# A hybrid decoder layer: pointwise and output weights joined, q stacked in halves of the partitions

## The chip, the cores and the metric

The kernel runs on one core of one Trainium2 chip. The metric is the device time of one execution in microseconds (us). The three runs of the kernel before took 2022.71, 2019.04 and 2021.59 us, a median of 2021.59. A core has five engines with a queue each: TensorE (PE, matmuls), VectorE (DVE), ScalarE (ACT), GpSimd (POOL) and SyncE (SP, which here only issues DMAs). ACT and POOL issue some DMAs as well.

## The reference

x is 2048 tokens by 1024 channels, float32. In short:

```python
hn   = rms_norm(x, mix_pre_g)
proj = hn @ w_in                     # q 512, k 128, v 128, conv input 2 x 512
attn = sliding_window_attention(q, k, v, sinks, rel_bias)   # 8 q heads, 2 kv heads of 64, window 128
h    = a * sigmoid(gate)             # conv input
h    = causal_depthwise_conv(h, 31 taps) + bias
conv = silu(layer_norm(h)) @ w_conv_pw                      # 512 x 512
mixed = concat(attn, conv) @ w_out                          # 1024 x 1024
h    = x + rms_norm(mixed, mix_post_g)
ff   = (silu(hn2 @ w_gate) * (hn2 @ w_up)) @ w_down         # hn2 = rms_norm(h), width 2816
out  = h + rms_norm(ff, ffn_post_g)
```

## The kernel before

**Matmuls.** Every large product is made of three matmuls. An operand is split into a high part (an ACT copy to the fp32r type, `act(w[:, 0], ...)`) and a low part (the difference, on DVE or POOL), and the product is high x high + high x low + low x high. The helper `three` (L188) issues them; `hl(tag)` (L64) makes a tile of 128 x 2 x 512 for the pair. All matmuls go through the helper `mat` (L107), so their profile line is L108; DVE operations go through `dve` (L83) and have line L85. Groups are therefore told apart by tile names: the letter after the @ is the stage.

**Stages.** Tokens are worked in four tiles of 512. For tile t:

- A (`stage_a`, L327): the input projection, 14 units of 24 matmuls each: eight for the conv input, then k (unit 8), v (9) and four pairs of q heads (10 to 13). Each unit loads 512 KB of w_in and, from tile 1 on, the stored low part (`lo_in`). k goes to `kz` (one buffer, high and low part of the last 128 and the present 512 tokens), q to `ql` tiles. The two kv groups lie in the two halves of the partitions.
- B (`stage_b`, L430): attention, four blocks of 128 tokens. For the scores, `front` issues twelve matmuls per block and pair of head pairs: 64 rows each, three products for each of two heads and two groups, the groups alternating between the two halves of the partitions. The sums lie in `tr` banks of PSUM.
- C (`stage_taps`, L563; `stage_tail`, L577; `conv_tail`, L592): 31 conv taps on DVE, then layer norm, swish and the pointwise product: the conv output is split (L618, L619), w_pw is loaded and split once per tile of tokens, 4 x 12 matmuls run in the single `ct` bank, and the result goes to `mixT` in DRAM by ACT's queue (L631).
- W (`stage_w`, L697): the output projection from `mixT` and w_out, then the norm and the residual (`norm_w`, L747).
- H, F, G: transposes and Strassen-like sums (`stage_h_sums`, L842) and the feed-forward (`stage_pre`, `stage_p1`, `stage_p2`) for two pairs of tiles.

**Order.** The tile framework schedules the instructions in a simulated time by priority (the written order) and sets all semaphores. Written order comes from generators. The main one runs stage after stage; beside it run lanes (`Lane`, L1275) that are given credit for each step of the main one: lb has attention, lc the taps, lw W0 and later C2, W2, C3, W3, ld the tails C0 and C1, lh the sums. A lane's entry can have a condition, such as a stage having started. In A1, hooks at certain units load the next tile's x, compute the row norms of tiles 2 and 3 (`row_norms`, L264, eight loads into `hl` buffers and eight ACT squares, hook at unit 2), turn the norm (L306, L308, tag `gb`) and split the next input (`split_x`, L311, units 10 and 11, eight `hl` tiles for tile 2).

**Buffers.** `BUFS` (L53) gives the buffers of each tag; a new tile waits until the tile that had its buffer is no longer read. Of interest here: wx 1, gb 2, hl 8, chl 5, fc 3, ql 4, w 6, raw 2; in PSUM mm 4, tr 3, ct 1.

Of the kernel before, what the change touches and what calls it, by code (L numbers as in the profile page):

```python
# [37 lines left out]
def layer_kernel(ctx, tc, x, xT, cols, rows, sinks, relb, onehot, w_in, w_pw, w_out, w_gate, w_up, w_down, out):  # L38
# [14 lines left out]
    BUFS = dict(x=4, p=4, wx=1, gb=2, hl=8, ql=4, chl=5, mid=4, mb=2, fa=4, at=2, fc=3, glu=2, yt=1, raw=2, w=6, vd=2)  # L53
# [10 lines left out]
    def hl(tag):  # L64
        return t_(tag, (P, 2, T), F32R)
# [165 lines left out]
    h_scr = dr.tile([S, D], F32, name="h_scr")  # L231

# [7 lines left out]
    kz = cst.tile([P, 2, P + T], F32R, name="kz")  # L240
    nc.gpsimd.memset(kz[:, :, 0:P].bitcast(F32), 0.0)
    junk = cst.tile([P, D], BF16, name="junk")
# [21 lines left out]
    def row_norms(ts, tag):  # L264
        lab[0] = f"A{ts[0]}"
        n = 4 * len(ts)
        ssq = sm(n)
        for i in range(n):
            xt = f4(tag)
            r0 = ts[0] * T + i * P  # L270
            nc.sync.dma_start(xt, x[r0 : r0 + P])
            act(junk, xt, AF.Square, accum_out=ssq[:, i : i + 1])
        r = rsqrt(ssq, n, D)
        for j, t in enumerate(ts):
            rn[t] = r[:, 4 * j : 4 * j + 4]
# [51 lines left out]
    def stage_a(t, hn, before_kv, hooks, post=None):  # L327
# [60 lines left out]
        if t:  # L388
            act(kz[:, :, 0:P], kz[:, :, T : T + P].bitcast(F32), AF.Copy)
# [4 lines left out]
        act(kz[:, 0, P:], ok, AF.Copy)  # L394
        vtt(kz[:, 1, P:], ok, kz[:, 0, P:].bitcast(F32), ALU.subtract)
# [11 lines left out]
        for i in range(4):  # L407
            oq = proj(10 + i)
            if i == 0:
                pv = mm()  # L410
                for s in range(4):
                    nc.tensor.transpose(pv[:, s * P : (s + 1) * P], vt[:, s * P : (s + 1) * P], ident)
                if t:
                    nc.vector.tensor_copy(vtok[:, 0], vtok[:, 4])
                nc.vector.tensor_copy(vtok[:, 1:5].rearrange("p a b -> p (a b)"), pv)
            qi = hl("ql")
            if post:
                qt = f2("fa")
                stt(qt, oq, 0.125, rb, ALU.mult, ALU.mult)
                act(qi[:, 0], qt, AF.Copy)  # L420
                vtt(qi[:, 1], qt, qi[:, 0].bitcast(F32), ALU.subtract)
            else:
                act(qi[:, 0], oq, AF.Copy, scale=0.125)
                stt(qi[:, 1], oq, 0.125, qi[:, 0].bitcast(F32), ALU.mult, ALU.subtract)
            q.append(qi)
            yield 5.2
            step(10 + i)
        qs[t] = q

    def stage_b(t):  # L430
# [3 lines left out]
        def front(b):  # L434
# [6 lines left out]
            for ip in range(2):  # L441
                os = [tr().rearrange("p (j k) -> p j k", j=2) for _ in range(2)]
                lead = []
                for j in range(2):
                    i = 2 * ip + j
                    for n, (a, k) in enumerate(((0, 0), (0, 1), (1, 0))):
                        for g in (1, 0):
                            sl = slice(64 * g, 64 * g + 64)
                            r = mat(os[g][:, j], q[i][sl, a, tok], kz[sl, k, win], start=n == 0, stop=n == 2)
                            if lead:  # L450
                                after_first(lead[-1], r)
                            if len(lead) < 2:
                                lead.append(r)
# [138 lines left out]
    def conv_tail(t, yt):  # L592
# [14 lines left out]
        sc = []  # L607
        for c in range(4):
# [8 lines left out]
            h = hl("chl")  # L617
            act(h[:, 0], v, AF.Copy)  # L618
            ptt(h[:, 1], v, h[:, 0].bitcast(F32), ALU.subtract)  # L619
            sc.append(h)  # L620
            yield 2
            lab[0] = L
        for m in range(4):
            raw = f2("fc")
            nc.sync.dma_start(raw, w_pw[m])
            w = split_w(raw, "mb" if t == 1 and m % 2 else "chl").rearrange("p a (k c) -> p a k c", c=P)
            o = ct()
            three(o, [((w[:, 0, k], w[:, 1, k]), (sc[k][:, 0], sc[k][:, 1])) for k in range(4)])
            z = f2("gb" if t > 1 else "fc")
            act(z, o, AF.Copy, scale=0.5)  # L630
            nc.scalar.dma_start(mixT[4 + m, :, t * T : (t + 1) * T], z)  # L631
            yield 2
            lab[0] = L
# [63 lines left out]
    def stage_w(w, spill, G, atag, htag, mtag, bank_of, norm=None, ready=None):  # L697
# [25 lines left out]
        for gi in range(KC // G):  # L723
            aa = nxt
            for n in range(2):
# [5 lines left out]
                ws = weight(w_out[2 * gi : 2 * gi + 2, :, n * T : (n + 1) * T].rearrange("c p t -> p c t"),  # L731
# [14 lines left out]

    def norm_w(w, spill, acc, mtag):  # L747
# [3 lines left out]
        ssq = sm(4)  # L751
# [4 lines left out]
        r = rsqrt(ssq, 4, D, w < 3)  # L756
        yield 3
        lab[0] = L
        ssq2 = sm(4)
        for s in range(4):  # L760
# [14 lines left out]
            act(junk, acc[s], AF.Square, accum_out=ssq2[:, s : s + 1])  # L775
            yield 5.0
        lab[0] = L
        r2 = rsqrt(ssq2, 4, D, w < 3)
# [586 lines left out]
    lw.add("W0", stage_w(0, True, 2, "x", "hl", "fa", mm), lambda: "A3" in started and "C0" in ld.done)  # L1365
    TGA = [["hl"] * 8, ["mid"] * 4 + ["chl"] * 4, ["hl"] * 8, ["mid"] * 4 + ["hl"] * 4]
# [138 lines left out]
```

## Time and profile before

| What | Value |
|---|---|
| Median of the runs | 2021.59 us |
| Profiled execution, first to last instruction (span) | 2016.4 us |
| Mean granted TensorE clock | 0.991 |
| Matmuls | 8826 |
| Moved by DMA | 451.44 MB, mean 224 GB/s |

The page gives no other time for the profiled execution than its span; what lies around it, by the median of the runs, is 5.2 us. Busy time is the union of an engine's records. A matmul's record is longer than its share of a dense stream, so the price of a matmul is taken from how many run in a stretch without a gap. In the view by groups the columns are: busy us, mean ns of one, idle us just before, and what ended the idle time. In the stretches each engine has its busy us and number of instructions, then come the granted clock, the share of the 16 DMA engines and GB/s. In the view of DMA issues the last two columns are KB each and us from issue to landing.

### The profile page before, as it was taken

To read this page: it belongs to the slowest core of one execution; us is meant where nothing else is said; L and a number is where in the kernel's file an instruction comes from. 1 tells how busy PE (TensorE), PEld (TensorE's weight loads), DVE (VectorE), ACT (ScalarE), POOL (GpSimd) and SP (SyncE) were. 2 spreads that over 40 slices of the span, in tenths; PEclk is the share of its full clock that TensorE was granted. 3 is DMA by queue.
4 is the path that set the end of the run, shared out by engine and by line. 5 is a ranking of instruction groups with operands and counts; after the bars stand their busy time and mean duration, and the time that the engine had idled before them with its cause. 6 is when DMAs were issued, how large, how long until landed. Compare 5 with 4: busy or idle time off the path is not lost. (4 is left out here: it accounts for less than half of the span.)

```text
span 2016.4 us, 27154 instructions
## 1 busy us (share of the span) xinstructions
PE 1957.8 (97%) x8826; PEld 1563.3 (78%) x8826; DVE 1489.5 (74%) x2679; ACT 985.7 (49%) x1938; POOL 355.0 (18%) x415
## 2 busy tenths in 40 slices
PE   8999999999998999999989999999899999999998
PEld 7877767677667778888878878778688888888886
DVE  5998987985794899888569984475766765545558
ACT  5455455457546633333355466456643343345543
POOL 6000223322110300000001022103523332221000
PEclk9999999999999999999989999999999999999999
DMA  8786645669559878777476778579944443366654
GB/s 309 267 298 221 207 148 175 194 228 322 180 178 325 281 238 269 253 253 254 149 239 216 238 261 283 173 262 348 333 159 167 157 160 107 107 238 214 200 187 162
DMA packets 234110, 451.44 MB, mean 224 GB/s; under 512 B 23496, under 2 KB 49264, under 8 KB 233968
## 3 DMA queue, kind: packets, MB, share of 16 engines
q1 hardware_dynamic: 211184, 411.96, 60.9%
q10 hardware_dynamic: 20544, 30.42, 4.1%
q0 software_dynamic: 2240, 7.34, 0.9%
q8 instruction: 69, 1.13, 0.2%
q14 instruction: 73, 0.60, 0.1%
HBM read 330.60 MB, written 119.02 MB: 223 GB/s over the span
## 5 line engine op out<-in xcount | busy, mean ns | idle before, releaser
L85 DVE SCALAR_TENSOR_TENSOR fc@C<-glu@C,colt,fc@C 128x512 f32<-128x512 f32 x480 | 367.8, 780 | 3.0
L108 PE MATMUL mm@F<-hl@H,w@F 128*128 128x512 f32 x1056 | 254.9, 392 | 5.3 <-ACT mm@F L924 4.9
L108 PEld LDWEIGHTS mm@F<-hl@H,w@F 128*128 128x128 f32 x1056 | 198.5, 189 | 48.8 <-ACT mm@F L924 6.7
L108 PE MATMUL mm@G<-hl@G,hl@G 128*128 128x512 f32 x924 | 228.0, 396 | 6.4 <-DVE x@G L85 4.3
L108 PE MATMUL mm@A<-hl@A,w@A 128*128 128x512 f32 x840 | 206.3, 396 | 3.0 <-ACT hl@A L318 1.2
L108 PEld LDWEIGHTS mm@G<-hl@G,hl@G 128*128 128x128 f32 x924 | 174.1, 190 | 44.5 <-issue 4.1
L797 ACT ACTIVATE w@F<-chl@F 128x512 fp32r<-128x512 f32 x220 | 135.6, 625 | 135.3 <-PE mm@F L108 123.3
L108 PE MATMUL mm@G<-w@G,hl@G 128*128 128x512 f32 x876 | 199.5, 389 | 0.0
L108 PEld LDWEIGHTS mm@G<-w@G,hl@G 128*128 128x128 f32 x876 | 164.4, 188 | 34.1
L108 PEld LDWEIGHTS mm@A<-hl@A,w@A 128*128 128x128 f32 x840 | 154.7, 188 | 39.4 <-DVE hl@A L85 3.0
L85 DVE TENSOR_TENSOR w@F<-chl@F,w@F 128x512 fp32r<-128x512 f32 x198 | 144.9, 733 | 34.7 <-ACT w@F L797 34.3
L108 PE MATMUL mm@F<-mid@H,w@F 128*128 128x512 f32 x528 | 131.1, 393 | 7.4 <-ACT mm@F L924 7.2
L108 PE MATMUL mm@F<-p@H,w@F 128*128 128x512 f32 x528 | 129.1, 389 | 0.8 <-ACT at@F L1046 0.8
L108 PE MATMUL mm@F<-ql@H,w@F 128*128 128x512 f32 x528 | 127.2, 389 | 0.7 <-ACT w@F L797 0.7
L108 PE MATMUL mm@F<-x@H,w@F 128*128 128x512 f32 x528 | 125.5, 391 | 0.0
L108 PEld LDWEIGHTS mm@F<-mid@H,w@F 128*128 128x128 f32 x528 | 98.3, 188 | 30.2 <-ACT mm@F L924 9.0
L108 PEld LDWEIGHTS mm@F<-p@H,w@F 128*128 128x128 f32 x528 | 98.9, 188 | 21.9 <-ACT at@F L1046 1.4
L108 PEld LDWEIGHTS mm@F<-ql@H,w@F 128*128 128x128 f32 x528 | 99.0, 188 | 21.6 <-ACT w@F L797 1.1
L108 PEld LDWEIGHTS mm@F<-x@H,w@F 128*128 128x128 f32 x528 | 98.7, 188 | 21.0
L108 PE MATMUL tr@W<-w@W,ql@W 128*128 128x512 f32 x384 | 103.0, 408 | 8.4 <-ACT ql@W L706 5.1
L133 ACT ACTIVATE w@A<-raw@A 128x512 fp32r<-128x512 f32 x110 | 67.7, 626 | 78.8 <-PE mm@A L108 51.5
L108 PE MATMUL mm@W<-w@W,hl@W 128*128 128x512 f32 x384 | 101.5, 404 | 2.2 <-ACT x@W L679 0.7
(302 smaller groups left out, 3337.0 us busy)
## 6 DMA issues: line engine op xcount, KB each, us to landing
mids<-fa@F SPq DMA_DIRECT2D x154, 256.0 KB, 2.7
raw@A<-w_in SPq DMA_DIRECT2D x55, 512.0 KB, 4.4
w@A<-lo_in SPq DMA_DIRECT2D x84, 256.0 KB, 3.5
fc@G<-mids SPq DMA_DIRECT2D x77, 256.0 KB, 3.5
fa@G<-mids SPq DMA_DIRECT2D x75, 256.0 KB, 4.5
gb@F<-keeps SPq DMA_DIRECT2D x72, 256.0 KB, 4.3
raw@W<-w_out SPq DMA_DIRECT2D x32, 512.0 KB, 5.5
w@W<-lo_out SPq DMA_DIRECT2D x48, 256.0 KB, 4.4
```

The source lines that it names most:

```text
L85: r = op(*args, **kw)
L108: r = nc.tensor.matmul(*args, **kw)
L133: act(w[:, 0], raw, AF.Copy)
L797: act(w[:, 0], x, AF.Copy)
```

## The change

Three things change, with what they need in buffers.

1. **Joined weights.** The conv output is no longer multiplied by w_pw tile by tile. A new stage J, in lane ld ahead of C0 and from the start of A1 on, computes 0.5 x w_pw x (rows 512 to 1023 of w_out) once, into `w_join` in DRAM; W reads it in place of these rows. The tails store the swish output itself in `mixT`, by SP's queue. (The host passes w_pw transposed.)
2. **Stacked q.** k and q are split into a staging tile and then copied by SP's DMAs: of each head of q the high part lies in partitions 0 to 63 and the low part in 64 to 127 (`qi`), and k is held in both halves (`kk`). A score is then two matmuls of 128 rows (k high, k low) instead of three of 64; it also contains low x low. The staging tiles use the tag wx (one buffer) for tiles 0 and 1 and chl for 2 and 3.
3. **Buffers.** chl has 4 instead of 5; `junk` has half the columns, so squares of 1024 columns come in two halves and their sums are added (`row_squares`).

```diff
-    BUFS = dict(..., chl=5, ...)
+    BUFS = dict(..., chl=4, ...)
...
+    w_join = dr.tile([4, P, D], F32, name="w_join")
...
-    kz = cst.tile([P, 2, P + T], F32R, name="kz")
+    kk = cst.tile([P, 2, 2, P + T], F32R, name="kk")
-    junk = cst.tile([P, D], BF16, name="junk")
+    junk = cst.tile([P, T], BF16, name="junk")
...
@@ row_norms
-            act(junk, xt, AF.Square, accum_out=ssq[:, i : i + 1])
+            act(xt, xt, AF.Square, accum_out=ssq[:, i : i + 1])
@@ stage_a, unit 8
-        act(kz[:, 0, P:], ok, AF.Copy)
-        vtt(kz[:, 1, P:], ok, kz[:, 0, P:].bitcast(F32), ALU.subtract)
+        kn = hl(TQ[t])
+        act(kn[:, 0], ok, AF.Copy)
+        vtt(kn[:, 1], ok, kn[:, 0].bitcast(F32), ALU.subtract)
+        for g in range(2):
+            for half in range(2):
+                nc.sync.dma_start(kk[64 * half : 64 * half + 64, g, :, P:].bitcast(F32), kn[64 * g : 64 * g + 64].bitcast(F32))
@@ stage_a, units 10 to 13
-            qi = hl("ql")
+            qn = hl(TQ[t])
...
+            qi = hl("ql")
+            for g in range(2):
+                for half in range(2):
+                    nc.sync.dma_start(qi[64 * half : 64 * half + 64, g].bitcast(F32), qn[64 * g : 64 * g + 64, half].bitcast(F32))
@@ stage_b, front
-                lead = []
-                for j in range(2):
-                    i = 2 * ip + j
-                    for n, (a, k) in enumerate(((0, 0), (0, 1), (1, 0))):
-                        for g in (1, 0):
-                            sl = slice(64 * g, 64 * g + 64)
-                            r = mat(os[g][:, j], q[i][sl, a, tok], kz[sl, k, win], start=n == 0, stop=n == 2)
...
+                for g in range(2):
+                    for j in range(2):
+                        for k in range(2):
+                            mat(os[g][:, j], q[2 * ip + j][:, g, tok], kk[:, g, k, win], start=k == 0, stop=k == 1)
@@ conv_tail
-            h = hl("chl")
-            act(h[:, 0], v, AF.Copy)
-            ptt(h[:, 1], v, h[:, 0].bitcast(F32), ALU.subtract)
-            sc.append(h)
+            nc.sync.dma_start(mixT[4 + c, :, t * T : (t + 1) * T], v)
             yield 2
             lab[0] = L
+
+    def stage_join():
+        lab[0] = "J0"
+        right = []
+        for k in range(4):
+            raw = f4("wx", (P, 2, T))
+            nc.sync.dma_start(raw, w_out[4 + k].rearrange("p (a b) -> p a b", a=2))
+            yield 1.5
+            for n in range(2):
+                lab[0] = "J0"
+                right.append(split_w(raw[:, n], "hl"))
+            yield 1.5
...
         for m in range(4):
-            raw = f2("fc")
+            if m % 2 == 0:
+                pair_ = t_("yt", (P, 2, 2, T), F32R)
+            raw = f2("gb")
             nc.sync.dma_start(raw, w_pw[m])
-            w = split_w(raw, "mb" if t == 1 and m % 2 else "chl").rearrange("p a (k c) -> p a k c", c=P)
-            o = ct()
-            three(o, [((w[:, 0, k], w[:, 1, k]), (sc[k][:, 0], sc[k][:, 1])) for k in range(4)])
-            z = f2("gb" if t > 1 else "fc")
-            act(z, o, AF.Copy, scale=0.5)
-            nc.scalar.dma_start(mixT[4 + m, :, t * T : (t + 1) * T], z)
...
+            left = split_w(raw, pair_[:, m % 2]).rearrange("p a (k c) -> p a k c", c=P)
+            yield 1.5
+            for n in range(2):
+                lab[0] = "J0"
+                o = ct()
+                three(o, [((left[:, 0, k], left[:, 1, k]), (right[2 * k + n][:, 0], right[2 * k + n][:, 1])) for k in range(4)])
+                z = f2("gb")
+                act(z, o, AF.Copy, scale=0.5)
+                nc.scalar.dma_start(w_join[m, :, n * T : (n + 1) * T], z)
+                yield 4
...
@@ stage_w
-                ws = weight(w_out[2 * gi : 2 * gi + 2, :, n * T : (n + 1) * T].rearrange("c p t -> p c t"),
+                src = w_out[2 * gi : 2 * gi + 2] if gi < 2 else w_join[2 * gi - 4 : 2 * gi - 2]
+                ws = weight(src[:, :, n * T : (n + 1) * T].rearrange("c p t -> p c t"),
...
@@ norm_w
+    def row_squares(x, ssq, s):
+        for n in range(2):
+            act(junk, x[:, n * T : (n + 1) * T], AF.Square, accum_out=ssq[:, 4 * n + s : 4 * n + s + 1])
...
-            act(junk, acc[s], AF.Square, accum_out=ssq[:, s : s + 1])
+            row_squares(acc[s], ssq, s)
...
@@ main
+    TQ = ["wx", "wx", "chl", "chl"]
...
+    ld.add("J", stage_join(), lambda: "A1" in started)
     for t in range(2):
         ld.add(f"C{t}", stage_tail(t), lambda t=t: since(lc, f"T{t}", CS))
```

More of the change, by code (lines that the diff above doesn't have):

```diff
@@ L51, in nm @@
         return f"{s}@{lab[0]}_{uid[0]}"
-    BUFS = dict(x=4, p=4, wx=1, gb=2, hl=8, ql=4, chl=5, mid=4, mb=2, fa=4, at=2, fc=3, glu=2, yt=1, raw=2, w=6, vd=2)
+    BUFS = dict(x=4, p=4, wx=1, gb=2, hl=8, ql=4, chl=4, mid=4, mb=2, fa=4, at=2, fc=3, glu=2, yt=1, raw=2, w=6, vd=2)
     def t_(tag, shape, dt=F32):
@@ L388, in stage_a @@
         if t:
-            act(kz[:, :, 0:P], kz[:, :, T : T + P].bitcast(F32), AF.Copy)
+            act(kk[:, :, :, 0:P], kk[:, :, :, T : T + P].bitcast(F32), AF.Copy)
         if post:
@@ L774, in norm_w @@
             nc.sync.dma_start(h_scr[r0 : r0 + P], acc[s])
-            act(junk, acc[s], AF.Square, accum_out=ssq2[:, s : s + 1])
+            row_squares(acc[s], ssq2, s)
             yield 5.0
         lab[0] = L
-        r2 = rsqrt(ssq2, 4, D, w < 3)
+        vtt(ssq2[:, 0:4], ssq2[:, 0:4], ssq2[:, 4:8], ALU.add)
+        r2 = rsqrt(ssq2[:, 0:4], 4, D, w < 3)
         yield 3
@@ L1479 @@
     wo = f(w_out)[np.concatenate([pair(i) for i in range(4)] + [np.arange(512, 1024)])]
-    wp = kblocks(f(w_conv_pw))
+    wp = kblocks(f(w_conv_pw).T)
     args = [
```

28 lines of the change are left out of this document (13 added, 15 removed).

## The prediction

> **What bounds the kernel now.** I read the page's head first, then busy time by stretches.
>
> ```profile
> span 2016.4 us, 27154 instructions
> PE 1957.8 (97%) x8826; PEld 1563.3 (78%) x8826; DVE 1489.5 (74%) x2679; ACT 985.7 (49%) x1938; POOL 355.0 (18%) x415
> ```
>
> ```profile
> core 0: us, PE busy (x) PEld busy (x) DVE busy (x) ACT busy (x) POOL busy (x), PEclk, DMA share, GB/s
> 95.50:120.00 24.50, 24.50 (x123) 18.36 (x122) 23.97 (x59) 15.38 (x37) 1.51 (x4) 1.00 1.02 389
> 120.00:192.00 72.00, 72.00 (x357) 55.21 (x357) 63.88 (x158) 33.56 (x87) 5.44 (x12) 1.00 0.73 236
> 192.00:309.00 117.00, 114.12 (x561) 84.40 (x560) 104.70 (x236) 63.39 (x168) 24.34 (x27) 0.99 0.55 175
> 473.00:533.00 60.00, 55.95 (x268) 38.18 (x266) 33.31 (x93) 39.66 (x90) 9.22 (x8) 0.97 0.66 228
> 1027.00:1290.00 263.00, 256.37 (x1131) 209.23 (x1132) 198.43 (x319) 145.82 (x258) 39.46 (x64) 0.99 0.73 240
> 1380.00:1460.00 80.00, 72.75 (x331) 58.85 (x331) 54.82 (x93) 51.28 (x98) 35.77 (x25) 1.00 0.98 349
> ```
>
> TensorE (PE) is busy 97% of the span: 58.6 us are idle in all. The stretches hold the second input stage (A1, 95.5 to 192), the third (A2), the conv tail of tile 1 beside W1 (473 to 533), the tails of tiles 2 and 3 beside W2 and W3 (1027 to 1290) and the feed-forward start with its DMA at 0.98 (1380 to 1460). PE is full or nearly full in each place where the change takes PE work away, so work taken from PE is time, as long as nothing new starves it. In A1 PE never rests, although the 16 DMA engines are saturated in its first 24.5 us; that is the place to watch. The price of a matmul comes from the chain and from PE's own timeline:
>
> ```profile
> 1451.94 343.02 PE mm@F L108 x1512
> ```
>
> ```profile
> 97.21 0.38 PE L108 MATMUL tr@B<-kz,ql@A 64*128 64x256 f32 x1
> 97.52 1.43 PE L108 MATMUL mm@A<-mid@A,w@A 128*128 128x512 f32 x5
> ...
> 112.68 0.97 PE L108 MATMUL tr@B<-kz,ql@A 64*128 64x256 f32 x12
> 113.58 2.56 PE L108 MATMUL mm@A<-chl@A,w@A 128*128 128x512 f32 x10
> ...
> 191.86 0.60 PE L558 MATMUL ct@C<-ident,fc@C 128*128 128x128 f32 x4
> 192.21 6.17 PE L108 MATMUL mm@A<-hl@A,w@A 128*128 128x512 f32 x26
> ```
>
> A full-array matmul of 512 columns takes 343.02 / 1512 = 0.227 us of PE in a dense stream; one of 128 columns (192.21 - 191.86) / 4 = 0.088. Durations of single records (about 0.39) overlap and are not used.
>
> **The change, part by part.**
>
> ```profile
> L108 PE MATMUL ct@C<-chl@C,chl@C 128*128 128x512 f32 x168 | 46.4, 417 | 1.8 <-ACT chl@C L133 1.2 <-POOL chl@C L135 0.6
> L108 PE MATMUL ct@C<-chl@C,mb@C 128*128 128x512 f32 x24 | 6.6, 410 | 0.7 <-POOL mb@C L135 0.6
> L108 PE MATMUL tr@B<-kz,ql@A 64*128 64x256 f32 x384 | 45.7, 310 | 0.1
> L85 DVE SCALAR_TENSOR_TENSOR fc@C<-glu@C,colt,fc@C 128x512 f32<-128x512 f32 x480 | 367.8, 780 | 3.0
> L619 POOL TENSOR_TENSOR chl@C<-fc@C,chl@C 128x512 fp32r<-128x512 f32 x16 | 24.8, 1548 | 106.3 <-ACT chl@C L618 95.3 <-PE ct@C L611 11.0
> L133 ACT ACTIVATE w@A<-raw@A 128x512 fp32r<-128x512 f32 x110 | 67.7, 626 | 78.8 <-PE mm@A L108 51.5 <-DMA raw@A<-w_in 20.1 <-DMA lo_in<-w@A 2.6
> ```
>
> *Pointwise product removed.* 192 matmuls go. Floor: 192 x 0.227 = 43.6 us. Ceiling: their busy and idle time, 46.4 + 1.8 + 6.6 + 0.7 = 55.5, because in the tails PE also waits for the splits on ScalarE (ACT) and GpSimd (POOL) inside these groups. I take 48, nearer the floor, since half of them lie in 1027 to 1290, where PE is busy for 256 of 263 us. The splits of the conv outputs and of w_pw, the 16 loads of w_pw and the scaled copies go too; ACT and POOL are under half busy, so this is nothing.
>
> *Join added.* 4 row blocks x 2 halves x 12 = 96 matmuls: 21.8 us by 0.227, 27.8 by 55.5 / 192 = 0.289. I take 23: A1 is a dense stream, but each chain uses the one ct bank. Net of both: 25 us less (16 to 34).
>
> *Scores.* 384 matmuls of 64 rows become 256 of 128 rows, 256 columns. Before: 45.7 us of PE. In a run of twelve, 113.58 - 112.68 = 0.90 us; one alone costs 0.31. After, each lies between half of 0.227 (0.113) and the line through 0.088 at 128 columns and 0.227 at 512 (0.134): 29 to 34 us; I take 0.12, so 31, nearer the half since PE streams at a constant rate per column. The 45.7 runs into the next matmul by 0.07 at the end of each run (0.97 against 0.90); with 32 runs or more that takes off some 2: a gain of 13 (10 to 15). Against twelve in a run, eight at 0.12 cost 0.96 and gain nothing; the gain lies in the broken runs.
>
> By the Trainium skill, "TensorE: Matmul & The Clock Gate", Part 3, matmuls in different row groups run at the same time, so 192 pairs should have cost 192 x 0.113 = 22 us and the full-array form, at 29, would lose 7; the row of twelve (0.15 per pair) bears this out only in part. "TensorEngine Tiling (Array Packing)", Tiling Modes, says that a change of tiling mode drains the engine, which fits the 0.31 of the single one and goes with the change.
>
> *Copies of q and k.* Each of 4 k and 16 q tiles now goes through a staging tile and four DMAs on the sync queue (SP): 80 issues, 12 MB.
>
> ```profile
> 90.97 0.33 SPq L271 DMA_DIRECT2D hl@A<-x  x1
> ...
> 93.72 1.78 SPq L132 DMA_DIRECT2D w@A<-lo_in  x1
> ```
>
> ```profile
> SPq L132 <- PE mm@A L108: 139.2, 61, 6.5
> ```
>
> ```profile
> raw@A<-w_in SPq DMA_DIRECT2D x55, 512.0 KB, 4.4
> hl@A<-x SPq DMA_DIRECT2D x8, 512.0 KB, 9.2
> mixT<-gb@C ACTq DMA_DIRECT2D x8, 256.0 KB, 4.1
> fc@C<-w_pw SPq DMA_DIRECT2D x16, 256.0 KB, 4.6
> ```
>
> An issue holds SP for 0.33 us: 20 per input stage are 6.6 us. SP already stands 139.2 us waiting for PE to free weight buffers, 46 in each of the three stages that load stored low parts, so it has room; what is queued behind a copy is the next weight loads, and PE holds up to two projections (11 us) in hand. The copies land 4.4 to 9.2 us later than the old in-place split; attention of a tile is a side lane of the next stage, which covers it. In tiles 0 and 1 the staging tile is a single buffer: copy, low part and landing, 0.63, at most a tap's 0.78 and 4.4, 5.8 us, against 24 x 0.227 = 5.4 per projection, and PSUM's four banks cover the difference. 16 stores of the conv output move from ACT's queue to SP (5.3 us of issues), less 12 loads of w_pw. Together I take a loss of 4 (0 to 12).
>
> *Norms.* The squares of W come in halves: 32 more ACT passes of about the split's 0.63, beside PE work; nothing, unless N3 is late, and its lane gets shorter by two tails.
>
> *The ring of hl in A1.* The join holds all eight hl buffers until its last chains; the row norms of tiles 2 and 3 use the same ring, and so does the split of A2's input.
>
> ```profile
> 94.39 1.04 ACT L272 ACTIVATE junk<-hl@A 128x1024 bf16<-128x1024 f32 x1
> ...
> 115.17 1.06 ACT L272 ACTIVATE junk<-hl@A 128x1024 bf16<-128x1024 f32 x1 [1.03 <-DMA hl@A<-x]
> ...
> 164.49 0.59 ACT L308 ACTIVATE gb@A<-mm@A 128x512 f32<-128x512 f32 x1
> 166.59 1.29 ACT L322 ACTIVATE hl@A<-x@A 128x512 fp32r<-128x512 f32 x2 [1.51 <-DVE x@A L85]
> ...
> 173.35 0.62 ACT L322 ACTIVATE hl@A<-x@A 128x512 fp32r<-128x512 f32 x1
> ```
>
> Now the split ends at 174 and A2 starts at 192: 18 us of slack. After, A1 ends at 192 + 22 - 3 = 211. The join: its first load needs the staging buffer, free after A0's last q copy, about 95.5 + 5.8 = 101; four w_out pairs, each a load (4.4), an ACT split (0.63) and two POOL subtractions (1.5 each, L619's row) = 8.0, end at 133. Four row blocks, each a load (4.6), a split (2.2), two chains with copies (2 x 3.3) and a store (4.1) that must land before the two-buffer gb ring turns, 14 to 17.5: the end at 189 to 203. With A2's eight splits (7.4) that is 196 to 211, just in time; but the loads fall into the saturated stretch, where landings cost 9.2, and the norm of A2 shares gb. I take 9 us of PE idle at A2's start (0 to 20).
>
> *One chl buffer fewer.* The Strassen sums before the feed-forward use three a step; the stall beside them is
>
> ```profile
> L108 PE MATMUL mm@F<-mid@H,w@F 128*128 128x512 f32 x528 | 131.1, 393 | 7.4 <-ACT mm@F L924 7.2
> ```
>
> 7.4 us over both pairs of tiles; a step that has to wait for a buffer adds to that. I take 4 more (0 to 8, the same again).
>
> **Sum.** -25 - 13 + 4 + 9 + 4 = -21 us on this execution's span of 2016.4, so 1995.4. The runs' median is 2021.59, 5.2 above the span; that stays: 2000.6, said as 2000.
>
> **The rivals.** *The norms stand behind the join.* If the join gets hl first, the row norms start only as it ends: 189 to 203, plus the eight squares (94.4 to 116.2, 21.8) and from the copied norm to the last split 164.5 to 174 (9.5): 220 to 234 against 211. The stall is about 20 instead of 9: 2011. For it: the join is first in the written order. Against it: the x rows are issued at 90.97, while A0 still runs, whenever a buffer frees, and the join's first split waits for the staging buffer.
>
> *Row groups already run side by side.* Then scores lose 7 instead of gaining 13: 2000 + 20 = 2020, no change. Against it stands 45.7, which is 0.24 per pair.
>
> *The copies hold the weights back (slower).* A copy waits in SP for the low part on VectorE (DVE), which stands behind conv taps.
>
> Two taps of 0.78, the low part and the ACT copy are 2.9 us; five tiles a stage, 14.5, plus 6.6 of issues, are 21, in four stages 84. SP's 46 us of standing in a stage cover this on average. The uncovered share decides: at 30% (25 of 84, the gain of 21 and the 4 already charged) the gain is gone. Half uncovered is 42 where the sum has 4: 38 more, 2038. For it: the DMA is saturated at A1's start. Against it: PE has weights for 11 us in hand, and one tile's hold is 2.9 + 4 x 0.33 = 4.2.
>
> **How the numbers follow.** Forecast 0.55, own range 1978 to 2010; norms behind the join 0.15; row groups 0.08; copies 0.22, a third of it in the partial form that only eats the gain. Faster: 0.55 + 0.15 + 0.03 of the row groups + 0.02 of the copies = 0.75. Within 0.2%, about what a measurement of this kernel can tell from no change: 0.05 + 0.03 = 0.08. Slower: 0.17. The range runs from 1978 (all terms at their good ends: -34 - 15 + 5 = -44) to 2030, which leaves out half of the slower case and a tail below.
>
> **What would show it.** PE's busy time falls by some 35 us; no group ct@C of 512 columns is left, and a group ct@J with x96 stands in A1 at about 0.23 us each; the scores' x256 take 29 to 34. The stretches 473 to 533 and 1027 to 1290 get shorter by about 12 and 22; A1 gets longer by 19. Idle time before A2's first matmul, put to an hl tile, shows the ring; the row norms' squares after the join's last chain would show the first rival. Idle PE in the input stages with a load of w@A or raw@A as releaser, while SP waits for a staging tile's low part, would show the copies. I am wrong if PE's busy time falls as said and the span doesn't.

## The result and the profile after

The changed kernel took 2041.35 us (median of four runs, 2035.98 to 2046.84) against 2022.15 of the kernel before beside it: a ratio of 1.0102, 95% interval 1.0080 to 1.0124. It is slower by some 20 us where 21 were to be gained, and lies outside the stated range of 1978 to 2030. The profiled execution took 2042.05 us, 1.75 more than its span.

The head of the page after, then PE and the other engines by stages, after and before (columns as in the prediction's stretches; a stage begins with the first matmul of its first product):

```profile
span 2040.3 us, 26960 instructions
...
PE 1936.2 (95%) x8602; PEld 1557.4 (76%) x8602; DVE 1501.6 (74%) x2687; ACT 979.1 (48%) x1974; POOL 325.5 (16%) x395
```

```profile
96.30:261.10 164.80, 130.50 (x565) 98.80 (x564) 119.30 (x252) 68.38 (x167) 28.00 (x30) 0.90 0.66 208
261.10:364.40 103.30, 100.00 (x482) 78.16 (x481) 82.17 (x205) 51.39 (x123) 7.05 (x17) 1.00 0.82 246
528.90:592.30 63.40, 43.70 (x195) 33.21 (x194) 49.55 (x129) 35.92 (x85) 7.73 (x14) 0.81 0.81 269
1059.50:1393.20 333.70, 318.71 (x1414) 260.82 (x1412) 254.08 (x450) 190.07 (x365) 30.07 (x75) 0.97 0.76 254
```

```profile
95.50:192.20 96.70, 96.70 (x481) 73.77 (x480) 88.05 (x216) 48.94 (x122) 6.96 (x15) 1.00 0.80 274
192.20:309.10 116.90, 114.02 (x560) 84.27 (x559) 104.60 (x236) 63.49 (x168) 24.34 (x27) 0.99 0.55 175
472.40:533.20 60.80, 56.75 (x271) 38.76 (x269) 33.51 (x94) 39.73 (x90) 9.61 (x10) 0.97 0.66 229
1006.40:1366.10 359.70, 344.05 (x1510) 280.37 (x1508) 261.92 (x440) 196.24 (x348) 46.57 (x79) 0.97 0.72 239
```

The rows are A1, A2, the stretch from A3's end to the feed-forward (with W1 and the tail of tile 1), and the tails of tiles 2 and 3 beside W2 and W3. A1 went from 96.7 to 164.8 us, 68 more. A2 gave 14 back: 24 matmuls of tile 0's pointwise product are gone from it, 24 of the attention moved ahead into A1, and the new form has 32 score matmuls fewer there. The stretch to the feed-forward has 76 matmuls fewer (271 to 195) and is still 2.6 us longer, with PE idle for 19.7 of 63.4. Only the last stretch paid: 26 less. PE's busy time fell by 21.6 (1957.8 to 1936.2) and its idle time grew from 58.6 to 104.1.

In A1 PE is idle for 34.3 us (164.8 - 130.5) and the granted clock is 0.90 where it was 1.00. The longest wait is on PE's own timeline; the squares of the row norms on ACT come before it, and before these the loads of their x rows on SP:

```profile
212.78 3.85 PE L108 MATMUL ct@J<-hl@J,yt@J 128*128 128x512 f32 x10 [0.95 <-POOL yt@J L135]
233.81 0.47 PE L307 MATMUL mm@A<-ident,gb@A 128*128 128x128 f32 x1 [17.17 <-DVE gb@A L85]
233.94 4.72 PE L108 MATMUL mm@A<-mid@A,w@A 128*128 128x512 f32 x12
238.49 1.55 PE L108 MATMUL mm@A<-chl@A,w@A 128*128 128x512 f32 x6
...
258.39 2.88 PE L108 MATMUL mm@A<-chl@A,w@A 128*128 128x512 f32 x12
261.11 1.07 PE L108 MATMUL mm@A<-hl@A,w@A 128*128 128x512 f32 x4
```

```profile
217.26 1.06 ACT L273 ACTIVATE hl@A<-hl@A 128x1024 f32<-128x1024 f32 x1 [6.21 <-DMA hl@A<-x]
...
228.26 1.06 ACT L273 ACTIVATE hl@A<-hl@A 128x1024 f32<-128x1024 f32 x1
```

```profile
213.31 9.82 SPq L272 DMA_DIRECT2D hl@A<-x  x8
```

The squares, which ran at 94.4 to 116.2 before, stand at 217.3 to 229.3: their x rows wait for the hl buffers that the join holds, and go out at 213.3, with the join's last chains (before: from 91.0 on). The transposes of the norm (`mm@A<-ident,gb@A`) wait for them, and A1's last projections, which need nothing of it, stand behind these transposes in PE's queue. The stall is thus not ahead of A2's first matmul (261.11 follows without a gap) but 17.17 us long inside A1.

Another 9.05 us of A1's idle time are waits for the copies of q (1.72, 4.47 and 2.86, all with `DMA ql@A<-wx@A` as releaser). ACT's writes into the staging tile of A0's four q tiles, one low part on DVE, and on SP a pair of copies and the first load that takes the tile over for the join:

```profile
86.00 0.63 ACT L425 ACTIVATE wx@A<-fa@A 128x512 fp32r<-128x512 f32 x1 [3.21 <-DMA kk<-wx@A]
100.27 0.63 ACT L425 ACTIVATE wx@A<-fa@A 128x512 fp32r<-128x512 f32 x1
117.72 0.63 ACT L425 ACTIVATE wx@A<-fa@A 128x512 fp32r<-128x512 f32 x1 [3.65 <-DMA ql@A<-wx@A]
124.96 0.63 ACT L425 ACTIVATE wx@A<-fa@A 128x512 fp32r<-128x512 f32 x1 [4.85 <-DMA ql@A<-wx@A]
```

```profile
102.45 0.68 DVE L85 TENSOR_TENSOR wx@A<-fa@A,wx@A 128x512 fp32r<-128x512 f32 x1
```

```profile
108.26 1.11 SPq L433 DMA_DIRECT2D ql@A<-wx@A  x2
...
134.88 0.33 SPq L627 DMA_DIRECT2D wx@J<-w_out  x1
```

One turn of the staging tile is (134.9 - 86.0) / 4 = 12.2 us against the 5.8 forecast, and the join starts at 135, not at 101. The second turn shows why: the low part is there at 103.1, SP comes to its copies only at 108.3, and the tile is free for ACT at 117.7. The groups of the new work, and how long PE waited before each:

```profile
L108 PE MATMUL tr@B<-kk,ql@A 128*128 128x256 f32 x256 | 48.1, 302 | 16.3 <-DMA ql@A<-wx@A 12.3 <-DVE sm@B L461 3.6 <-DMA ql@A<-chl@A 0.3
L108 PE MATMUL ct@J<-hl@J,yt@J 128*128 128x512 f32 x96 | 27.5, 421 | 2.9 <-ACT yt@J L133 1.9 <-POOL yt@J L135 0.9
```

### The profile page after: what moved, and what is told of

Its sections match the earlier page's. It is cut to its first block, busy times and chain, and to the rows that moved or that the text cites. A ratio compares the mean times of both kernels' runs of the same rounds, so it can differ in the third digit from the quotient of the medians.

```text
span 2040.3 us, 26960 instructions
## 1 busy us (share of the span) xinstructions
PE 1936.2 (95%) x8602; PEld 1557.4 (76%) x8602; DVE 1501.6 (74%) x2687; ACT 979.1 (48%) x1974; POOL 325.5 (16%) x395
## 4 chain that ended last, share of the span: by engine, by line
PE 51%; DVE 6%; DMA 5%; issue 2%; ACT 1%; POOL 0%; SPq 0%; DVEq 0%; ACTq 0%; POOLq 0%
PE mm@F L108 32%; PE mm@G L108 16%; PE tr@W L108 3%; DVE fc@C L85 1%; DMA mids<-fa@F 1%; DVE hl@G L85 1%; DVE w@F L85 1%; DVE fa@F L85 1%; DMA mixT<-fc@C 1%; DVE mid@W L85 1%; DMA at@W<-mixT 1%; DMA gb@F<-keeps 1%; DMA hT<-gb@H 0%; DVE chl@F L85 0%; DMA wx@G<-w_down 0%
## 5 line engine op out<-in xcount | busy, mean ns | idle before, releaser
L85 DVE TENSOR_TENSOR w@F<-chl@F,w@F 128x512 fp32r<-128x512 f32 x198 | 151.5, 768 | 56.8 <-ACT w@F L822 56.7
L108 PE MATMUL tr@W<-w@W,ql@W 128*128 128x512 f32 x384 | 98.7, 400 | 4.2 <-ACT ql@W L724 2.8
```

Source lines behind the costliest of these rows:

```text
L85: r = op(*args, **kw)
L108: r = nc.tensor.matmul(*args, **kw)
```

## The experiments

Theory after the result: three things take more than the removed matmuls give. The ring of hl puts the norm behind the join (the first rival); the copies cost far more than 4 us (the slower rival); and half of the pointwise product was never worth its PE time. The rival to the last: the product was worth it, and what new work follows hides that. Ratios are to the kernel before on the same chip; 0.001 is 2.0 us.

### What the pointwise product is worth

```diff
 conv_tail, all tiles (e1) or tiles 0 and 1 alone (e12)
-            h = hl("chl") ...                 # split, load and split of w_pw, 4 x 12 matmuls, scaled copies
+            nc.sync.dma_start(mixT[4 + c, :, t * T : (t + 1) * T], v)
```

> The kernel before with the pointwise product left out altogether (the swish output goes to mixT, W reads w_out as it is; so a part of the computation is missing). It prices the removed 192 matmuls in the whole kernel. My price, 43.6 to 55.5 us of PE, gives 1968 to 1978. If the tails' matmuls were hidden beside other waits the time falls by less than 30.

> The kernel before without the pointwise product for tiles 0 and 1 alone (96 of the 192 matmuls; a part of the computation is missing). By PE's price that is 96 x 0.227 = 22 us less, 0.989. By e1's stretches nothing is gained there: the start of the feed-forward stays at 533 to 537 us and the ratio at 0.997 to 1.002.

Measured: e1 0.9882 (0.9840 to 0.9925), 24 us; e12 1.0008 (0.9988 to 1.0027). So the 96 matmuls of tiles 0 and 1 are worth nothing, and the other 96, in the tails beside W2 and W3, all the 24 us: in e1 the feed-forward's first matmul is at 535.1 (before 533.2), and only 1006.4 to 1366.1 shrank, from 359.7 to 335.2. What PE did with the freed time stands in one pair of stretches of before and of e12, with equal bounds:

```profile
303.00:475.00 172.00, 170.91 (x810) 125.90 (x809) 144.86 (x299) 92.71 (x221) 56.25 (x84) 1.00 0.67 222
475.00:535.00 60.00, 55.95 (x266) 38.36 (x265) 35.31 (x98) 37.66 (x88) 8.90 (x8) 0.97 0.62 216
```

```profile
303.00:475.00 172.00, 160.43 (x747) 117.10 (x746) 145.64 (x305) 84.66 (x204) 46.84 (x67) 0.96 0.63 198
475.00:535.00 60.00, 49.17 (x213) 32.06 (x212) 45.55 (x116) 33.29 (x80) 7.64 (x14) 0.89 0.73 247
```

It idled: it was busy for 209.6 of 232 us instead of 226.9. What PE waits for there in e12, by its list of waits (engine and tile, the tile's writer: us in total, times, longest):

```profile
PE tr@B L108 <- DVE sm@B L459: 6.2, 2, 4.8
PE mm@W L108 <- ACT hl@W L711: 4.9, 1, 4.9
PE tr@H L820 <- DVE sm@B L459: 3.7, 1, 3.7
```

In the kernel before, the longest of these waits was 2.5 us. By these waits the attention's softmax (`sm@B` on DVE) and the chain behind it through W1 and its norm set the end of this stretch just beside PE, and the pointwise product of tiles 0 and 1 filled PE's waits for it. That is argued from the waits. It fits that e11 below, which shortens the scores, a link of this chain, starts the feed-forward 25 us earlier than e1 (509.8 against 535.1). By the Trainium skill, "Perfetto Trace Analysis", Identifying the Most-Contended Engine, the share of time in which the matmul engine is busy is a poor measure of how near it is to its limit. The outcome here fits that: at 97% busy, 96 matmuls fewer, 22 us at 0.227 each, changed nothing.

### The join and the ring of hl

e3 is the changed kernel with the scores as before (k and q unsplit over the halves, no copies). e5 has, in addition, the row norms of tiles 2 and 3 in A0, in other buffers, as e4 has in the changed kernel. e8 is e3 with the join in A2 and in other buffers.

```diff
 e4, e5: A0's hook
-                row_norms([t] if t == 1 else [2, 3], "p" if t == 1 else "hl")
+                row_norms([1], "p")
+                row_norms([2, 3], "p")
 e4, e5: A1's hooks
-                hooks = {0: h1, 2: h0, 7: h2, ...}
+                hooks = {0: h1, 7: h2, ...}
 e8: the join's lane and buffers
-    ld.add("J", stage_join(), lambda: "A1" in started)
+    lw.add("J", stage_join(), lambda: "A2" in started)
-                right.append(split_w(raw[:, n], "hl"))
+                right.append(split_w(raw[:, n], "mid" if k < 2 else "chl"))
-            left = split_w(raw, pair_[:, m % 2])
+            left = split_w(raw, "mb")
```

> The changed kernel with the scores as before (kz, three products of 64 rows, no copies), the join kept. Theory R: the norms still stand behind the join, A1 stays above 140 us and the time is 2015 to 2040. Theory C: the join alone is harmless, A1 is about 120 us, the time 1995 to 2005.

> The join alone (scores as before) with the row norms of tiles 2 and 3 in A0, so without q's copies and without the ring. e3, the same with the ring, took 2034 and had 16.5 us of idle PE in front of the norm's transposes in A1 (163 us long). If the ring is what the join costs beyond its 22 us of matmuls, A1 falls to 118 to 130 us and the time to 2000 to 2015. If the join costs by something else (its splits on POOL, its stores, the one ct bank), A1 stays at 140 or more and the time at 2025 or more.

> The join in A2 instead of A1, in buffers that are free there (mid and chl for the parts of w_out, mb for w_pw), scores as before. e1 shows that taking the tails' matmuls out of A2 to W1 moves the start of the feed-forward by nothing, so PE has room there, and that 24 us are gained in the stretch of W2 and W3. If so, the join's 22 us of matmuls are hidden in A2 and A3 and the time is 1995 to 2008, below both kernels. If PE has no room, 2015 to 2025.

Measured: e3 1.0070 (1.0048 to 1.0092), e5 0.9966 (0.9951 to 0.9981), e8 1.0034 (1.0013 to 1.0055). The group of the norm's transposes on PE, in e3 and in e5, and e5's A1:

```profile
L307 PE MATMUL mm@A<-ident,gb@A 128*128 128x128 f32 x12 | 2.2, 289 | 16.5 <-DVE gb@A L85 16.5
```

```profile
L307 PE MATMUL mm@A<-ident,gb@A 128*128 128x128 f32 x12 | 2.2, 291 | 0.3 <-DVE gb@A L85 0.3
```

```profile
96.00:224.00 128.00, 125.50 (x602) 93.60 (x601) 113.79 (x240) 57.69 (x149) 25.43 (x18) 1.00 0.66 210
```

The stall goes with its cause: 16.5 us of waiting to 0.3, and 21 us of the time (1.0070 - 0.9966). The ring is shown, in a kernel without the copies; in the kernel before, A1 has no idle time that earlier norms could save (96.70 busy of 96.70). What is left of the join, with the smaller chl and the halved squares, costs 17 us over e1 (0.9966 - 0.9882), somewhat less than its PE work. In A2 the join was expected to be hidden, and it is not: e8 stands 31 us over e1 (1.0034 - 0.9882), A2 takes 159.1 us instead of e1's 109.5, and PE is idle for 16.5 of them (in an execution 9 us above e8's median). What it costs there beyond its matmuls was not taken apart.

### The scores' form and the copies

e11 is e1 with the new form of the scores, read straight from the split k and q: no staging tile and no copies. e2 is the changed kernel without the join (W reads w_out itself), so e1, pointwise product missing, with the whole second part of the change and the smaller buffers.

```diff
 e11: stage_b, front, in the kernel of e1
+                            mat(os[g][:, j], q[2 * ip + j][:, g, tok], kz[:, k, win], start=k == 0, stop=k == 1)
 e2: the changed kernel
-    ld.add("J", stage_join(), lambda: "A1" in started)
-                src = w_out[...] if gi < 2 else w_join[...]
+                src = w_out[2 * gi : 2 * gi + 2]
 e6: e2 with two staging tiles in stages 0 and 1
-            qn = hl(TQ[t])
+            qn = hl(("wx", "mb")[i % 2] if t < 2 else "chl")
 e7: e2 with the 80 copies on POOL's queue
-                    nc.sync.dma_start(qi[...], qn[...])
+                    nc.gpsimd.dma_start(qi[...], qn[...])
```

> e1 (no pointwise product) with the new form of the scores, 256 matmuls of 128 rows, but read straight from the split k and q, without copies, staging or second keys; the scores are then of a wrong arrangement, their cost is that of the new form. It prices the form by itself against e1's 0.988 of the kernel before. The prediction's price: 13 us less, 0.982. If the scores are not what PE's queue waits for, it is within 4 us of e1: 0.986 to 0.990. By the row groups running side by side it would be 7 us more, 0.992.

> The changed kernel without the join (stage J is not run, W reads w_out; the pointwise product is missing). Against e1 it shows the stacking of q, the copies and the smaller buffers alone. Theory R (the ring of hl in A1 holds the row norms behind the join): without the join the ring is free, so this is within 10 us of e1, A1 about 97 to 102 us long. Theory C (the copies of q and k on SP's queue and the single staging buffer hold the kernel): 25 us or more slower than e1, A1 110 us or longer.

> e2 (stacked q, no join, no pointwise product; a part of the computation is missing) with a second staging buffer for k and q of tiles 0 and 1. In e2 one turn of the single buffer took 13 us (copy at 84.6, 98.0, 120.9, 133.8) against 5.4 us per projection, and A1 was 24 us longer than in e1. If the single buffer is the cause, A1 falls from 121 to about 100 to 108 us and the time from 2012 to 1995 to 2003. If SP's queue or the DMA load is, nothing moves by more than 5.

> e2 with the 80 copies of q and k issued by POOL's queue in place of SP's, where they no longer wait behind weight loads that wait for PE (the single staging buffer stays; the pointwise product is missing). In e2 a copy stood up to 8 us between the low part's end and its issue. If SP's order is the cause, a turn of the buffer falls from 13 to 6 to 8 us, A1 to 100 to 108 and the time to 1995 to 2003. If the buffer's number alone is, it stays at 2008 or more.

Measured: e11 0.9713 (0.9683 to 0.9743), e2 0.9967 (0.9948 to 0.9985), e6 0.9922 (0.9899 to 0.9945), e7 0.9972 (0.9950 to 0.9993). The form alone gains 34 us over e1 (0.9882 - 0.9713), more than any of the three expectations, and the copies with all that goes with them take 51 back (0.9967 - 0.9713). e2's 17 us over e1 lie between the bounds of the two theories; its A1 of 120.6 us is theory C's. A second staging tile returns 9, another queue nothing. The heads of e1 and e11:

```profile
PE 1924.0 (97%) x8634; PEld 1533.0 (77%) x8634; DVE 1475.6 (74%) x2679; ACT 960.7 (48%) x1890; POOL 309.8 (16%) x383
```

```profile
PE 1896.6 (97%) x8506; PEld 1532.4 (78%) x8506; DVE 1478.2 (76%) x2679; ACT 960.0 (49%) x1890; POOL 313.3 (16%) x383
```

PE's busy time falls by 27.4 us. Counted from the start of each record to the next, idle time left out, the scores take 41.6 us in e1 and 35.0 in e11, only 6.6 less. More lies in their neighbours. The first two lines are of e1, the last two of e11; in both a single matmul of the input projection stands between two runs of scores:

```profile
103.78 0.49 PE L108 MATMUL mm@A<-mid@A,w@A 128*128 128x512 f32 x1
104.21 0.38 PE L108 MATMUL tr@B<-kz,ql@A 64*128 64x256 f32 x1
```

```profile
111.11 0.40 PE L108 MATMUL mm@A<-chl@A,w@A 128*128 128x512 f32 x1
111.34 0.63 PE L108 MATMUL tr@B<-kz,ql@A 128*128 128x256 f32 x4
```

It takes 104.21 - 103.78 = 0.43 us in e1 and 0.23 in e11. At full clock, the projection's matmuls just before and just after a run of scores take 0.33 us on average in e1 and 0.23 in e11, all others 0.23 in both. So it is each border between the 64-row form and the full one that costs, about 0.1 us on either side. "TensorEngine Tiling (Array Packing)", Key Properties, in the Trainium skill says that a change of the tiling mode drains the engine. The slower neighbours fit that; no record shows the drain itself. Part of the 27.4 us goes with the granted clock, 0.990 over the span instead of 0.983.

Three kernels then ask what about the copies costs. To e11 they add the 80 copies of k and q into something that nobody reads, so that no score waits for them: whole, through one wx buffer (e14); the same with 8 columns instead of 512 (e16); whole, each to a place of its own in DRAM, so that none waits for the landing of an earlier one (e17).

```diff
+            qd = dead("q")                    # e14, e16: hl("wx"); e17: its own part of a DRAM tile
+            for g in range(2):
+                for half in range(2):
+                    nc.sync.dma_start(qd[64 * half : 64 * half + 64, g], qi[64 * g : 64 * g + 64, half])   # e16: [..., 0:8]
```

> e11 with the 80 copies of q and k issued as in the changed kernel by SP, but into a buffer that nobody reads; the scores still come from the split tiles (wrong arrangement, no pointwise product). If the load on SP and the DMA engines is what costs, most of the 50 us is back: 0.988 or more. If it is the wait for the copies, this stays within 0.005 of e11: 0.968 to 0.976.

> The kernel before without the pointwise product, with scores of 128 rows read straight from the split k and q (wrong arrangement), plus the 80 copies of k and q into a buffer that nobody reads, each copy with 8 columns in place of 512: the issues, SP's waits for the low parts and the turn of the buffer stay, nearly all of the 12 MB goes. Without copies that kernel had 0.9713, with the whole copies 0.995. If the order in SP's queue and its waits are the cost, this stays within 0.005 of 0.995; if the transferred bytes are, it falls to 0.971 to 0.976; in between, both count.

> The same kernel, the 80 copies whole (12 MB), but each to a place of its own in DRAM that nobody reads: the bytes, the issues and SP's wait for the low part stay, the wait for the landing of the copies before goes. If SP's wait for the landing is the cost, this falls to 0.971 to 0.98; if the bytes or the wait for the low part are, it stays at 0.99 or above.

Measured: e14 0.9950 (0.9928 to 0.9972), e16 0.9836 (0.9805 to 0.9868), e17 0.9782 (0.9744 to 0.9820). Nearly all of e2's loss is there although no score waits for a copy: 48 us. Without the bytes 25 are left, without the wait for the landing 14 (here the copies also go to DRAM instead of on-chip memory, which was not tested by itself). A1, and the stretch from A3's end to the feed-forward, in e11, e14, e16 and e17:

```profile
95.30:190.60 95.30, 95.11 (x454) 74.97 (x453) 87.57 (x220) 53.27 (x142) 11.02 (x16) 1.00 0.79 271
...
452.80:509.80 57.00, 43.15 (x210) 34.29 (x209) 40.38 (x107) 39.99 (x88) 3.78 (x12) 0.85 0.74 256
```

```profile
97.10:209.30 112.20, 101.99 (x472) 79.59 (x471) 97.73 (x235) 55.68 (x147) 9.15 (x18) 0.94 0.88 269
...
477.50:547.00 69.50, 42.84 (x199) 32.83 (x198) 51.26 (x127) 37.92 (x87) 7.01 (x14) 0.78 0.77 260
```

```profile
97.20:193.90 96.70, 94.89 (x453) 75.03 (x452) 88.14 (x219) 52.67 (x141) 7.83 (x16) 1.00 0.81 262
...
460.70:530.20 69.50, 43.93 (x206) 34.98 (x205) 48.36 (x121) 42.88 (x93) 7.20 (x25) 0.78 0.67 228
```

```profile
94.70:199.00 104.30, 97.42 (x462) 77.37 (x461) 94.84 (x229) 52.46 (x140) 5.06 (x16) 0.97 0.83 273
...
463.10:532.00 68.90, 45.15 (x199) 34.69 (x199) 49.80 (x129) 35.97 (x83) 5.68 (x14) 0.80 0.76 251
```

The bytes cost in A1, where the DMA share is 0.88 in e14 against 0.79 in e11: 112.2 and 104.3 us with them, 96.7 without, 95.3 with no copies. The later stretch is 12 longer in all three, so there the bytes and the landing are not the cause. Among PE's waits in it, those of the transposes `tr@H` for their load of hn_scr, which SP issues, are longer than in e11: 19.5 us in e14, 8.7 in e16 and 10.3 in e17 against 6.0. What is common to the three is 80 issues in SP's queue, each behind its low part, and the order of instructions that the scheduler planned with them. Which of these two it is stays open.

Part of each difference lies where no copy and hardly a score runs. From the feed-forward's first matmul to the end of the tails, 793.7 us pass in e11, 807.1 in e1, and 808.4, 809.7 and 804.2 in e14, e16 and e17. In its first part, up to the feed-forward's second half, the same 2034 matmuls take 465.6 us in e11 and 477.3 in e4 below, with PE idle for 7.9 and 16.1 of them. So 13 of the form's 34 us, and 10 to 16 of what the copies cost, cannot be tied to scores or copies; what makes e11 quicker there is not shown. Besides, the profiled execution of e11 took 1954.8 us against a median of 1961.3, that of e17 1988.2 against 1977.7.

SP's waits for a landing and its copies from issue to landing, first in e14 and then in e16:

```profile
SPq L434 <- DMA wx@A<-ql@A: 18.2, 16, 2.9
```

```profile
wx@A<-ql@A SPq DMA_DIRECT2D x64, 128.0 KB, 5.0
```

```profile
SPq L434 <- DMA wx@A<-ql@A: 4.9, 7, 1.5
```

```profile
wx@A<-ql@A SPq DMA_DIRECT2D x64, 2.0 KB, 2.8
```

Bytes and landing go together: a whole copy lands after 5.0 us instead of 2.8, and SP stands 18.2 us instead of 4.9 until the buffer is free, with the weight loads behind it.

### The mends in the changed kernel

e4 is the changed kernel with the early norms (diff above), e9 with the second staging tile, e10 with both.

> The changed kernel with the row norms of tiles 2 and 3 moved to A0, in the four p buffers that are free there, so that they share nothing with the join. Theory R: A1 falls from 165 to 120 to 135 us and the time to 1995 to 2010. Theory C: A1 stays above 150 and the time above 2025, since q's copies and the staging buffer are as they were.

> The changed kernel whole, with a second staging buffer for k and q of tiles 0 and 1, the ring of hl as it was. With e10 and e4 it makes a square of ring and staging. If the two losses are separate (staging 9 us by e6 against e2, ring 21 by e5 against e3), this is at 2028 to 2035; if each hides the other, it stays at 2036 to 2042, because the norms still come behind the join.

> The changed kernel with both mends: row norms of tiles 2 and 3 in A0 and a second staging buffer. Separate losses: 2041 - 21 - 9 = 2011. If the staging hid the ring in e4 (7 us only), the two together give more than the sum of the single mends: 2008 to 2018, A1 125 to 132 us. If something else in the changed kernel holds A1, it stays at 2025 or more.

Measured: e4 1.0067 (1.0037 to 1.0097), e9 1.0127 (1.0097 to 1.0158), e10 1.0005 (0.9989 to 1.0021). The early norms gain 7 us alone and 25 beside the second tile; the second tile gains nothing alone (the interval of e9 overlaps that of the changed kernel) and 12 beside the early norms. e4 lies between its two theories (2032.8 us, A1 143.2) and e9, at 2045.5, above both. By the ratios either loss hides the other; the profiles show that only in part. In e4 A1 is down from 164.8 to 143.2 us and the feed-forward starts 20 us earlier (572.0 instead of 592.3), but the stretch from there to its second half takes 477.3 us instead of 467.2, so half of the gain is gone again. In e10 A1 is only 4 us shorter than in e4 (139.3); 11 of the 12 us lie in that later stretch (466.2), whose matmuls are the same. A gain or loss of some 10 us in one of these kernels can come from there.

### Without the copies

ACT and DVE can write the halves themselves: an operand in partitions 0 to 63, its result in 64 to 127. e13 is e2, and e15 is e4, with that in place of staging tile and copies. e15 computes all of the layer.

```diff
-            qn = hl(TQ[t])
-            act(qn[:, 0], oq, AF.Copy, scale=0.125)
-            stt(qn[:, 1], oq, 0.125, qn[:, 0].bitcast(F32), ALU.mult, ALU.subtract)
             for g in range(2):
-                for half in range(2):
-                    nc.sync.dma_start(qi[64 * half : 64 * half + 64, g].bitcast(F32), qn[64 * g : 64 * g + 64, half].bitcast(F32))
+                src = oq[64 * g : 64 * g + 64]
+                act(qi[0:64, g], src, AF.Copy, scale=0.125)
+                stt(qi[64:128, g], src, 0.125, qi[0:64, g].bitcast(F32), ALU.mult, ALU.subtract)
```

> e2 (no join, no pointwise product: a part of the computation is missing) with the stacked q and the double k written straight by ACT and DVE into the other half of the partitions: no copies, no staging, 7 more ACT and 7 more DVE operations a tile. If the copies are the loss, this comes near e11: 0.970 to 0.978. If the loss sits in the 128-row operands or the bigger key buffer (its carry-over copy, one buffer for all tiles), it stays at 0.990 or more.

> The whole computation: join in A1, row norms of tiles 2 and 3 in A0, scores in the stacked form written by the engines without copies. From e5 (0.9966) and the gain of the form alone (e11 against e1, 0.017 less) I expect 0.978 to 0.984, about 1980 us, below both kernels. If the copies were not the loss: 0.995 or more.

Measured: e13 0.9835 (0.9819 to 0.9852), 27 us under e2; e15 0.9910 (0.9895 to 0.9926), 1999.50 us, 32 under e4 and 18 under the kernel before. Both take longer than was expected, by 0.0055 and 0.007 beyond the upper bounds. Still, the two ideas of the change pay together, without the copies and with the norms moved. The new writes of q on the two engines in e15:

```profile
L85 DVE SCALAR_TENSOR_TENSOR ql@A<-mm@A,ql@A 64x512 fp32r<-64x512 f32 x24 | 16.5, 689 | 2.9 <-ACT ql@A L430 2.2
L430 ACT ACTIVATE ql@A<-mm@A 64x512 fp32r<-64x512 f32 x24 | 14.2, 593 | 13.8 <-DVE ql@A L85 7.1 <-PE mm@A L108 6.4
```

They take 0.69 and 0.59 us for 64 rows, twice as many instructions as before. Against e11, with none of them, e13 stands 25 us higher, but by the profiles 16 of these lie between the feed-forward's start and the end of the tails (809.7 against 793.7), where none of the writes stands.

## Why the prediction was wrong

*Pointwise product removed (48 taken, 24 measured).* The price per matmul was right, the place was not: "PE is full or nearly full in each place where the change takes PE work away, so work taken from PE is time" failed. It held beside W2 and W3 (forecast 22 for that stretch, measured 24) and not at all ahead of the feed-forward, where the other half of the 48 was expected, 12 of it in the stretch from 473 to 533 (measured: 0 for both tiles together, e12). By the waits, PE and the softmax chain on DVE ended together there, and 97% busy didn't tell one from the other. The quoted row of 473 to 533 with DVE at 33 of 60 us even pointed away from DVE: it would be the length of the chain, not its load; that is argued, not shown.

*Join added (23 taken).* Near: 27.5 us of the group's records, at the forecast's ceiling of 27.8, and 17 us of time where the ring is out of its way (e5).

*Scores (13 taken, 34 measured).* Each was priced at 0.12 us, and a run of eight takes that:

```profile
144.07 1.11 PE L108 MATMUL tr@B<-kk,ql@A 128*128 128x256 f32 x8
145.02 1.32 PE L108 MATMUL mm@A<-chl@A,w@A 128*128 128x512 f32 x5
```

That is 0.95 / 8. Over the whole trace, though, the scores themselves gave only 6.6 us of PE's time, half of the 13. What was left out is the full-array matmuls beside each run (0.33 us instead of 0.23 in e1); and 13 of the 34 us lie behind the feed-forward's start, where they are not explained. The sign given for this step, 29 to 34 us of the group, was a poor one: the group reads 48.1, since records overlap at each end of a run. The rival "row groups already run side by side" is refuted in its outcome by e11, which is faster and not 7 us slower; that they overlap in part the row of twelve had shown.

*Copies of q and k (4 taken; 48 to 51 measured against no copies at all, 27 and 32 against writes by the engines).* This step failed most: "together I take a loss of 4 (0 to 12)". Its term "5.8 us" for a turn of the staging tile was 12.2, since SP comes late to the copies and their landing meets a busy DMA. The rival "the copies hold the weights back" was the case; its mechanism was right in part. It named SP's wait for the low part; e14 and e17 show that the wait for a landing, made long by the bytes, costs more (34 us between them) than the rest (14). That its 2038 lies near the 2041 is luck: the other terms of its sum were off as well, the pointwise product by 24, the ring by 12 and the scores by 21 the other way.

*The ring of hl (9 taken, 21 measured in e3 and e5).* The first rival came about, with a wait of 17.17 us against its "about 20". It was ranked second for a wrong reason: the x rows, issued at 90.97 before, were taken to go out as early after; they went out once the join let go of the buffers. It also costs A1's own projections, behind the transposes in PE's queue, which no step had.

*One chl buffer fewer (4 taken).* Not tried alone. The stretch from the feed-forward's start to its second half is 6 us shorter after (467.2 against 473.2), so no loss is seen there. But that stretch differs by as much between kernels with the same buffers (e4 and e10), so it shows nothing small.

By "I am wrong if PE's busy time falls as said and the span doesn't": it fell by 21.6 of the 35, and the span rose by 23.9. The terms measured apart add up to -24 + 17 - 34 + 51 + 21 = +31 against the +20 of the whole; they overlap, as the mends show. The 5.2 us between span and median that the sum adds at its end is no part of the miss: in the runs here about 1.8 us lie around the span, so the rest is how much quicker the profiled execution was than the median.

## What to carry to other kernels

Work taken from an engine is time only where that engine alone ends the stretch; at 97% busy, leave the work out in one stretch alone and see. Price a copy between parts of the on-chip memory by the turn of its staging buffer at the landing times of the busy stretch, and by what stands behind it in its queue, not by its issue; where an engine that already writes the tile can write it to the right partitions, let it. When a buffer ring gets a second user, look for the work of the first that is late next, and for what stands behind that work on an in-order engine.

## What the runs showed of the hardware

After the idle 17.17 us, twelve matmuls took 238.49 - 233.94 = 4.55 us, and later ones 261.11 - 258.39 = 2.72. The granted clock is 0.50 from 220.6 to 237.6, so until 3.8 us after the work begins again, and 1.00 behind that. By the Trainium skill, "TensorE: Matmul & The Clock Gate", Part 1, an idle array falls to half its clock and takes about 3.4 us of work to come back. By an estimate from that figure this would lose 1.7 us; the trace agrees with 1.8. A long wait of PE thus costs more than its length.

A matmul of the input projection just before or after a run of 64-row scores took 0.33 us at full clock, the others 0.23 (e1).

ACT and DVE write a result into the other half of the partitions than the one that holds their operand (e15), at 0.59 and 0.69 us for 64 rows of 512 columns.

Copies issued on POOL's queue instead of SP's (e7) changed nothing in the time: 0.9972 against 0.9967.
